# Gate modulation sums tied behind the Strassen sums written ahead of them, and branch B's second factors tied behind attention's output stores

## The chip, the cores and the metric

The kernel runs as one program on one core of one Trainium2 chip. The metric is the device time of one execution in microseconds (us); the median of the runs shown is compared. The engines named below are PE (matrix products), DVE (vector work), ACT (activations, copies), POOL (vector work as well) and SP, which here only issues transfers.

## The reference

One layer of a transformer-like block is computed on 1024 positions of width 1024, all in float32. What matters here, cut down:

```python
c_act = jax.nn.silu(c)
mod = c_act @ ada_w[l] + ada_b[l]
sh1, sc1, g1, sh2, sc2, g2 = jnp.split(mod, 6, axis=-1)
h = rmsnorm(x, ln1_g[l]) * (1.0 + sc1) + sh1
p = h @ w_in[l]
q, k, v, cb, cc, cx, ga, gb = jnp.split(p, split_at, axis=-1)
...
y_a = stick_breaking_attention(q, k, v)
y_b = cb * causal_dwconv(cc * cx, conv_w[l])
merged = (jax.nn.sigmoid(ga) * (y_a @ w_branch_a[l])
          + jax.nn.sigmoid(gb) * (y_b @ w_branch_b[l]))
x = x + g1 * (merged @ w_out[l])
h = rmsnorm(x, ln2_g[l]) * (1.0 + sc2) + sh2
...
x = x + g2 * f
```

The change concerns two things: where in time four of the six vectors of `mod` are summed (they are used only after attention: `g1`, `sh2`, `sc2`, `g2`), and when `y_b` is read back for its product with `w_branch_b`.

## The kernel before, in words

**The gate stage.** Six of the eight parts of `p` (q, cc, cx, cb, gb, ga) are computed here in 24 rounds, called gates here, by one loop (L671 to L745). A gate computes two blocks of 128 output rows by 1024 positions. It uses Strassen's scheme: seven products `p1` to `p7` take the place of eight. Each product is 12 matmuls of 128x512 (L131 to L133: a high part and a low part of each float32 weight), so a gate is 84 matmuls. PE takes them strictly in the order written: p1, p2, p6, p5, p7, p3, p4. The gates run in the order `gates` (L466): section 5 (q) four times; then for each j of 0 to 3 the sections 1, 2 and 0 (cc, cx, cb); then section 4 (gb) four times and section 3 (ga) four times. Counted from 0, gate 13 is section 1 with j=3, and gates 16 and 17 are the first two of section 4.

For each gate SP loads two weight tiles `raw` and `raw2` of 512 KB (L451). POOL makes four combinations of them, `ws` (L136 as a helper, and L682), and ACT and DVE split each factor in two: ACT writes the high part `whi` (L462), DVE the low part `wlo` (L136). The seven products land in PSUM buffers `pj`, of which there are six; DVE adds them up to the four outputs, tiles `c` (L136, the Strassen sums `c11`, `c12`, `c21`, `c22`). A PSUM buffer comes free when its sum has been made. In section 0 the result is multiplied with the convolution's output on POOL and written out by ACT in two parts, `ybt` (L655 to L658).

**The modulation sums.** The generator `mods_later` (L539 to L583) computes the four vectors. Each vector takes eight loads of 512 KB, `ad` (L550), and for each load one DVE instruction that multiplies and sums along the row into a column of `msum` (L565, followed by a short read of the accumulator). The loads are written up to three ahead of the sums, and a quota per gate limits them; their buffers have the tags `tr` and `sq`, two each, shared with `yt`, `ybt` and others of the same gates. After the eight sums of the vector of section 2 (`g1`) and of section 5 (`g2`), DVE adds a bias (`msum += gcol`, L571), and PE spreads the result over the partitions by 16 small matmuls (L578). For the two other vectors DVE writes `mod`. The loop calls `step()` (L660) after each Strassen output: `later()` follows c11, c22, c12 and c21, and in section 1 there is a fifth call at the end of the gate.

The instructions of one engine are issued in an order that a scheduler works out from the written order and its own estimate of when each operand is ready. Before the change a sum may therefore stand on DVE wherever the scheduler believes that its load has landed, also ahead of Strassen sums that were written before it.

**The attention stage.** Per head and block of 128 queries PE computes scores `z` (L846, L847), ACT their sigmoid, DVE a scan `pt` (L856), PE transposes, ACT and DVE split these into `ath` and `atl`, and PE multiplies with v into `o` (L885). ACT writes `o` to an `oy` tile (L889, four buffers), and SP stores it in two transfers to `d_ya` (L893). The factors of each head are loaded by SP in six transfers (L782 to L784: `sqt`, `skh`, `skl`). Between attention's steps PE runs other products as fillers, among them branch B's `y_b @ w_branch_b` (L946 to L948). Its second factors are loaded back in two halves of positions by `load_yb(0)` and `load_yb(1)` (L952 to L959): each makes eight loads of 512 KB `big<-d_yb` on SP. They are written inside `tc.issue_after(lastz[0].ins)`: after the last score matmul written so far.

Of the kernel before, what the change touches and what calls it, by code (L numbers as in the profile page):

```python
# [12 lines left out]
ALU = mybir.AluOpType  # L13
# [9 lines left out]
DH = 64  # L23
# [7 lines left out]
def block_kernel(tc, x, x_t, cols, ada_1, ada_2, ada_row, w_q, w_kv, w_v1, w_cg, w_a, w_b, w_o, w_g, w_u, w_d, out):  # L31
    nc = tc.nc
# [100 lines left out]
            nc.tensor.matmul(ps, wl[:, k, :], fh[:, k, :], start=False, stop=(k == 3))  # L133

    def tt(eng, out, a, b, op):
        eng.tensor_tensor(out=out, in0=a, in1=b, op=op)  # L136


    psA = ExitStack()
# [253 lines left out]
    ml = factors()  # L393
# [40 lines left out]
    for e in range(3):  # L434
        n = d_v[e].shape[0]
# [105 lines left out]
    def mods_later():  # L541

        cab = gp.tile([P, D], F32, name="cabg")
        todo, ahead = [(q, k) for q in range(len(SECS)) for k in range(KT)], ads_

        def load_next():
            if todo and quota[0] > 0:
                quota[0] -= 1
                ad = gp.tile([P, D], F32, tag=("tr", "sq")[len(todo) % 2], bufs=2, name=nm("ad"))
                nc.sync.dma_start(ad, ada_2[todo.pop(0)])  # L550
                ahead.append(ad)

        nc.sync.dma_start(cab, ada_row[0:1, :].broadcast_to([P, D]))
        cs_ = gp.tile([P, D], F32, tag="tr", bufs=2, name=nm("cs"))
        nc.scalar.activation(cs_, cab, AF.Sigmoid)
        for n in range(2):
            tt(nc.vector, cab[:, n * 512:n * 512 + 512], cab[:, n * 512:n * 512 + 512], cs_[:, n * 512:n * 512 + 512], ALU.mult)
        yield
        for q, sec in enumerate(SECS):
            ms = gp.tile([P, 8], F32, tag="msum", bufs=2, name=nm("msum"))  # L560
            for k in range(KT):
                while len(ahead) < 3 and todo and quota[0] > 0:
                    load_next()
                ad = ahead.pop(0)
                nc.vector.tensor_tensor_reduce(out=ad, in0=ad, in1=cab, scale=1.0, scalar=0.0, op0=ALU.mult,  # L565
                                               op1=ALU.add, accum_out=ms[:, k:k + 1])
                yield
            if sec in (3, 4):
                tt(nc.vector, mod[:, sec - 1], ms, acol[:, sec - 1], ALU.add)
                continue  # L570
            e = 0 if sec == 2 else 1  # L571
            tt(nc.vector, ms, ms, gcol[:, e], ALU.add)
            yield
            gb_ = gp.tile([P, D], F32, tag="tr", bufs=2, name=nm("gb"))
            for n in range(2):
                ps = g_ss()
                for i in range(4):
                    nc.tensor.matmul(ps[:, i * P:(i + 1) * P], ms[:, 4 * n + i:4 * n + i + 1].broadcast_to([P, P]), ident,  # L578
                                     start=True, stop=True)
                nc.scalar.activation(gb_[:, n * 512:(n + 1) * 512], ps, AF.Copy)  # L580
            nc.scalar.dma_start(d_g[e], gb_)
            yield
# [77 lines left out]
    def step():  # L660
        if (quota[0] or ads_) and ml_begun:
            ml_begun.append(1)
            next(ml, None)

    uc, ys = {}, {}
    pend, pmm, eq = [], [], end_q()
    with tc.high_priority(), tc.issue_after(last_raw[0].ins):
        nc.sync.dma_start(ft[6].bitcast(F32), d_t[6])
    for g, (sec, j) in enumerate(gates):
        raw, raw2 = raws  # L670
        if g == 7:  # L671
            next(ml)
            ml_begun.append(1)
        p1, p2 = pre[g] if g in pre else (g_prod(g_split(raw[:, :512]), 0), g_prod(g_split(raw[:, 512:]), 1))
        a11, a12, a21, a22 = raw[:, :512], raw[:, 512:], raw2[:, :512], raw2[:, 512:]
        s1, s2_, s3, s4 = (gp2.tile([P, 512], F32, tag=f"ws{q}", bufs=1, name=nm("ws")) for q in range(4))
        with tc.high_priority() if g == 0 else ExitStack():
            tt(nc.gpsimd, s3, a11, a21, ALU.subtract)
            tt(nc.gpsimd, s2_, a22, s3, ALU.subtract)
            w6 = g_split(s2_)  # L680
        tt(nc.gpsimd, s1, a21, a22, ALU.add)
        ws4 = nc.gpsimd.tensor_tensor(out=s4, in0=a12, in1=s2_, op=ALU.subtract)  # L682
        if g + 1 < len(gates):
            raws = two_raw(g + 1)
        c11, c21, c12, c22 = (gp.tile([P, 512], F32, tag=f"c{q}", bufs=2, name=nm("c")) for q in range(4))

        def put(c, m, n):
            if sec == 5:
                pend.append((c, m, n))
            elif sec > 2:  # L690
                nc.scalar.activation(c, c, AF.Sigmoid)
                nc.scalar.dma_start((d_sga, d_sgb)[sec - 3][m, :, n * 512:(n + 1) * 512], c)
            elif sec == 0:
                put_b(c, m, n)
            elif sec == 1:
                ccs[m, n] = c
            elif n == 1 and m >= 4:
                ccs["late"] = c
            else:
                put_u(c, m, n)  # L700
                if n == 0 and m >= 4:
                    put_u(ccs["late"], m, 1)

        quota[0] = (4 if j else 0) if sec == 1 else 3 if sec in (3, 4) and g + 1 < len(gates) else 0
        turn = [0]

        def later():
            if sec == 1 or sec in (3, 4) and turn[0] > 0:
                step()
            turn[0] += 1  # L710
            if len(pmm) > 1 or pmm and not pend:
                sum_q(*pmm.pop(0))
            if pend:
                put_q(*pend.pop(0))
            elif g > 3 and not pmm:
                with tc.issue_after(ws4.ins):
                    next(eq, None)

        nc.scalar.activation(c11, p1, AF.Copy)
        p4 = g_prod(g_split(a22), 3) if g + 1 == len(gates) else None  # L720
        p6 = g_prod(w6, 5)
        tt(nc.vector, c21, p6, c11, ALU.add)
        tt(nc.vector, c11, p2, c11, ALU.add)
        put(c11, j, 0)
        later()
        p5 = g_prod(g_split(s1), 4)
        tt(nc.vector, c12, p5, c21, ALU.add)
        p3 = g_prod(g_split(s4), 2) if g == 0 else None
        p7 = g_prod(g_split(s3), 6)
        tt(nc.vector, c22, p7, c12, ALU.add)  # L730
        put(c22, j + 4, 1)
        later()
        tt(nc.vector, c21, p7, c21, ALU.add)
        p3 = p3 or g_prod(g_split(s4), 2)
        tt(nc.vector, c12, p3, c12, ALU.add)
        put(c12, j, 1)
        later()
        p4 = p4 or g_prod(g_split(a22), 3)
        tt(nc.vector, c21, p4, c21, ALU.add)
        later()  # L740
        put(c21, j + 4, 0)
        if g + 1 == len(gates):
            for _ in eq:
                pass
        if sec == 1:  # L745
            step()
        if g + 1 == len(gates):
            quota[0] = 99
            for _ in ml:
                pass  # L750
# [74 lines left out]
    lastz = [None]  # L825
# [52 lines left out]
    def att_av(h, g):  # L878
        pr, e0 = h // 2, (h % 2) * DH
        vt = vts[h]  # L880
        o = pps.tile([P, 256], F32, tag="o", bufs=1, name=nm("o"))
        for j in range(2 * g + 2):
            c0 = P if j == 2 * g + 1 else 0
            th, tl = ats[h, g, j // 4]
            nc.tensor.matmul(o[:, c0:], vt[:, j, :], th[:, j % 4, c0:], start=(j == 0), stop=False)  # L885
            lastav[0] = nc.tensor.matmul(o[:, c0:], vt[:, j, :], tl[:, j % 4, c0:], start=False, stop=(j == 2 * g + 1))
        yv = bp.tile([P, 256], F32, tag="oy", bufs=4, name=nm("oy"))
        for e in range(2):
            nc.scalar.activation(yv[:, e * P:(e + 1) * P], o[:, e * P:(e + 1) * P], AF.Identity,  # L889
                                 bias=vlast[:, h, 2 * g + e:2 * g + e + 1])  # L890
        hf, c0 = g // 2, (g % 2) * 256
        for e in range(2):
            nc.sync.dma_start(d_ya[hf][pr, e0:e0 + DH, e, c0:c0 + 256], yv[e * DH:(e + 1) * DH])  # L893
        yield None

    NZ, NTR, NPJ, DAV, KQ = 2, 3, 2, 4, 1
# [44 lines left out]
    def mm_ch(ps, w, ah, al, k0=0, k1=KT):  # L941

        for k in range(k0, k1):
# [3 lines left out]
            nc.tensor.matmul(ps, wh, rl_, start=False, stop=False)  # L947
            nc.tensor.matmul(ps, wl, rh_, start=False, stop=(k == KT - 1))  # L948

    yh, yl = [], []  # L950

    def load_yb(n):  # L952
        yh.append(big())
        yl.append(big())
        for k in range(0, KT, 2):
            for e, t in enumerate((yh, yl)):
                with tc.issue_after(lastz[0].ins):
                    nc.sync.dma_start(t[n][:, k:k + 2].bitcast(F32), d_yb[e][n][:, k:k + 2])
                yield  # L959

# [63 lines left out]
    def fill(to):  # L1024
        nonlocal tf
        while tf < to:
            d_ = next(fl, None)
            if d_ is None:
                break
            tf += d_  # L1030
# [630 lines left out]
```

## Time and profile before

| what | value |
|---|---|
| median of 3 runs (lowest to highest) | 1830.23 us (1827.88 to 1831.91) |
| the profiled execution, its own time | 1838.09 us |
| its span in the trace | 1836.3 us |
| mean granted PE clock | 0.994 |
| PE, DVE, ACT, POOL busy, share of the span | 98%, 74%, 43%, 28% |
| SP's transfers (queue q1) | 302.76 MB, 50.7% of 16 DMA engines |
| loads `ad<-ada`, L550 | x32, 512 KB each, 4.6 us to landing (median) |
| loads `raw<-w_cg`, L451 | x40, 512 KB each, 3.8 us to landing (median) |

The profile is of one execution; 1.8 us of its time lie outside the span, and it took 7.9 us more than the median of the runs. Rows of a timeline begin with the start and the duration in us; a bracket at the end names how long the engine had been idle and what released it. In a table of windows each engine has its busy time and, in brackets, the instructions that began in that window; the three last columns are the granted clock of PE, the busy share of the DMA engines and GB/s.

### The profile page before, as it was taken

The page shows a single profiled execution, that of the slowest core. Times are in us where ns is not written, and L with a number is a line of the kernel's source. Part 1 is how long each engine was busy: PE and PEld are TensorE (multiplying, and loading weights), DVE is VectorE, ACT ScalarE, POOL GpSimd, SP SyncE. Part 2 cuts the span into 40 slices and gives each one's busy share as a digit, 9 for nine tenths or more (in the row PEclk, how much of TensorE's full clock was granted, in tenths as well). Part 3 has the DMA queues.
Part 4 walks back from the last instruction along what each step waited for, and adds up shares of the span by engine and source line. Part 5 has one row for each costly group of instructions (what it writes and reads, how often), then busy time and mean ns, then how long its engine had stood idle before and what let it go on. Part 6 is the DMA issues. An engine that isn't in the chain of part 4 may idle for free. (4 is left out here: it accounts for less than half of the span.)

```text
span 1836.3 us, 24702 instructions
## 1 busy us (share of the span) xinstructions
PE 1794.5 (98%) x8781; PEld 1498.3 (82%) x8781; DVE 1352.1 (74%) x1882; ACT 793.9 (43%) x1510; POOL 505.5 (28%) x362
## 2 busy tenths in 40 slices
PE   7999999999989999899999999999999999999999
PEld 4788778878878899788887888877888888878887
DVE  7873877988896448788998655589977788644776
ACT  3452553333334347677776321663444344422321
POOL 0043338533333211342221000105544454200000
PEclk9999999999989999999999999999999999999999
DMA  9687542344484388887775646424534344299876
GB/s 395 196 320 293 184 138 74 119 140 149 129 295 138 118 253 227 255 212 189 176 172 161 231 149 217 134 94 154 204 138 149 129 171 171 104 331 345 283 230 219
DMA packets 164018, 357.48 MB, mean 195 GB/s; under 512 B 15976, under 2 KB 65456, under 8 KB 161720
## 3 DMA queue, kind: packets, MB, share of 16 engines
q1 hardware_dynamic: 133880, 302.76, 50.7%
q10 hardware_dynamic: 29008, 49.48, 7.3%
q0 software_dynamic: 1008, 3.67, 0.5%
q8 instruction: 70, 1.15, 0.3%
q14 instruction: 52, 0.43, 0.1%
HBM read 245.22 MB, written 110.66 MB: 194 GB/s over the span
## 5 line engine op out<-in xcount | busy, mean ns | idle before, releaser
L856 DVE TENSOR_TENSOR_SCAN pt<-pt,mk 128x896 f32<-128x896 f32 (+7 forms) x128 | 189.4, 1480 | 14.5 <-ACT pt L848 14.5
L131 PE MATMUL pj<-big,whi 128*128 128x512 f32 x384 | 150.9, 393 | 2.5 <-DVE c L136 2.5
L133 PE MATMUL pj<-big,wlo 128*128 128x512 f32 x384 | 150.1, 391 | 0.0
L132 PE MATMUL pj<-big,whi 128*128 128x512 f32 x384 | 150.1, 391 | 0.0
L136 DVE TENSOR_TENSOR c<-pj,c 128x512 f32<-128x512 f32 x168 | 111.7, 681 | 43.1 <-PE pj L133 42.8
L136 POOL TENSOR_TENSOR ws<-raw,raw 128x512 f32<-128x512 f32 x44 | 60.8, 1381 | 297.8 <-DMA raw<-w_cg 144.7
L131 PE MATMUL e<-big,whi 128*128 128x512 f32 x352 | 137.5, 391 | 2.0 <-ACT c L1388 1.4
L133 PE MATMUL e<-big,wlo 128*128 128x512 f32 x352 | 137.0, 389 | 0.0
L132 PE MATMUL e<-big,whi 128*128 128x512 f32 x352 | 137.0, 389 | 0.0
L136 DVE TENSOR_TENSOR c<-e,c 128x512 f32<-128x512 f32 x138 | 92.9, 687 | 52.7 <-PE e L133 51.7
L874 DVE TENSOR_TENSOR atl<-tr,ath 128x512 fp32r<-128x512 f32 (+1 forms) x192 | 99.3, 543 | 34.9 <-ACT ath L873 34.6
L1488 PE MATMUL e<-whi,f 128*128 128x512 f32 (+1 forms) x319 | 121.8, 382 | 1.0 <-DMA f<-d_f 1.0
L1489 PE MATMUL e<-wlo,f 128*128 128x512 f32 (+1 forms) x319 | 121.8, 382 | 0.0
L1490 PE MATMUL e<-whi,f 128*128 128x512 f32 (+1 forms) x319 | 121.6, 382 | 0.0
L133 PE MATMUL pj<-ft,wlo 128*128 128x512 f32 x288 | 113.4, 394 | 4.3 <-DVE wlo L136 4.3
L848 ACT ACTIVATE pt<-z,rq 128x512 f32<-128x512 f32 (+1 forms) x192 | 105.0, 584 | 24.6 <-PE z L847 24.4
L131 PE MATMUL pj<-ft,whi 128*128 128x512 f32 x288 | 113.5, 394 | 1.8 <-ACT whi L462 1.6
L132 PE MATMUL pj<-ft,whi 128*128 128x512 f32 x288 | 113.0, 393 | 0.0
L308 PE MATMUL pj<-whi,big 128*128 128x512 f32 x352 | 109.4, 396 | 3.6 <-ACT big L291 3.6
L136 DVE TENSOR_TENSOR wlo<-ws,whi 128x512 fp32r<-128x512 f32 x96 | 84.3, 887 | 31.1 <-ACT whi L462 29.0
L462 ACT ACTIVATE whi<-raw 128x512 fp32r<-128x512 f32 x112 | 69.7, 629 | 86.2 <-PE pj L132 49.1
L132 PE MATMUL e<-rl,whi 128*128 128x512 f32 x264 | 103.3, 391 | 2.2 <-DVE rl L136 2.2
(262 smaller groups left out, 4866.0 us busy)
## 6 DMA issues: line engine op xcount, KB each, us to landing
f<-d_f SPq DMA_DIRECT2D x77, 512.0 KB, 3.6
d_f<-fs SPq DMA_DIRECT2D x70, 512.0 KB, 3.2
raw<-w_cg SPq DMA_DIRECT2D x40, 512.0 KB, 3.8
ad<-ada SPq DMA_DIRECT2D x32, 512.0 KB, 4.6
raw<-w_u SPq DMA_DIRECT2D x26, 512.0 KB, 3.4
raw<-w_g SPq DMA_DIRECT2D x25, 512.0 KB, 3.7
ada<-ada SPq DMA_DIRECT2D x8, 1024.0 KB, 9.6
d_t<-ts SPq DMA_DIRECT2D x16, 512.0 KB, 8.1
```

What stands on the lines that cost most here:

```text
L131: nc.tensor.matmul(ps, wh[:, k, :], fh[:, k, :], start=(k == 0), stop=False)
L132: nc.tensor.matmul(ps, wh[:, k, :], fl[:, k, :], start=False, stop=False)
L133: nc.tensor.matmul(ps, wl[:, k, :], fh[:, k, :], start=False, stop=(k == 3))
L136: eng.tensor_tensor(out=out, in0=a, in1=b, op=op)
L308: nc.tensor.matmul(ps, a, b, start=(k == 0 and q == 0), stop=(k == KT - 1 and q == 2))
L462: nc.scalar.activation(hi, src, AF.Copy)
L848: nc.scalar.activation(pt[:, off + s0:off + s0 + m], z[:, :m], AF.Sigmoid, scale=rq[:, 1, i, h:h + 1])
L856: nc.vector.tensor_tensor_scan(out=pt[:, rev], data0=pt[:, rev], data1=mk[:, rev], initial=1.0, op0=ALU.mult, op1=ALU.max)
L874: nc.vector.tensor_tensor(out=tl[:, :nb, c0:c0 + P], in0=src, in1=th[:, :nb, c0:c0 + P].bitcast(F32), op=ALU.subtract)
L1488: nc.tensor.matmul(o, sh, w[0][:, c], start=(j == 0), stop=False)
L1489: nc.tensor.matmul(o, sh, w[1][:, c], start=False, stop=False)
L1490: nc.tensor.matmul(o, sl, w[0][:, c], start=False, stop=(j == NJ - 1))
```

## The change

First, `step()` runs the next piece of `mods_later` inside `tc.issue_after(at[0].ins)`, where `at[0]` is the Strassen sum written last before the call. Each DVE instruction of that piece now stands behind that sum in DVE's order. The loads are also written at another place: a load is written after the sum that makes room for it, not ahead of the next one. Second, the loads of `load_yb(1)` are tied behind the last store of attention's output that is written (`lastya`, L893), not behind the last score matmul; `load_yb(0)` has no tie any more.

```diff
 def mods_later():
...
+        def fill():
+            while len(ahead) < 3 and todo and quota[0] > 0:
+                load_next()
...
             for k in range(KT):
-                while len(ahead) < 3 and todo and quota[0] > 0:
-                    load_next()
+                if not ahead:
+                    fill()
+                    yield
                 ad = ahead.pop(0)
                 nc.vector.tensor_tensor_reduce(out=ad, in0=ad, in1=cab, scale=1.0, scalar=0.0, op0=ALU.mult,
                                                op1=ALU.add, accum_out=ms[:, k:k + 1])
+                fill()
                 yield
...
 def step():
         if (quota[0] or ads_) and ml_begun:
             ml_begun.append(1)
-            next(ml, None)
+            with tc.issue_after(at[0].ins):
+                next(ml, None)
...
-        tt(nc.vector, c11, p2, c11, ALU.add)
+        at[0] = tt(nc.vector, c11, p2, c11, ALU.add)
...
-        tt(nc.vector, c22, p7, c12, ALU.add)
+        at[0] = tt(nc.vector, c22, p7, c12, ALU.add)
...
-        tt(nc.vector, c12, p3, c12, ALU.add)
+        at[0] = tt(nc.vector, c12, p3, c12, ALU.add)
...
-        tt(nc.vector, c21, p4, c21, ALU.add)
+        at[0] = tt(nc.vector, c21, p4, c21, ALU.add)
...
-            nc.sync.dma_start(d_ya[hf][pr, e0:e0 + DH, e, c0:c0 + 256], yv[e * DH:(e + 1) * DH])
+            lastya[0] = nc.sync.dma_start(d_ya[hf][pr, e0:e0 + DH, e, c0:c0 + 256], yv[e * DH:(e + 1) * DH])
...
 def load_yb(n):
...
-                with tc.issue_after(lastz[0].ins):
+                with tc.issue_after(lastya[0].ins) if n else ExitStack():
                     nc.sync.dma_start(t[n][:, k:k + 2].bitcast(F32), d_yb[e][n][:, k:k + 2])
```

Three places show what this does to the order of the instructions. In the changed kernel L565 is L570, L571 is L577, L578 is L584, and L893, L958 are L900, L966.

The first place is DVE in gate 16, the first gate of section 4. Before, its rows are (`ad` and `msum` are the modulation sums, `c` the Strassen sums, `wlo` the low parts of weights):

```order
L565 ISA ad_4295,msum_3825<-ad_4295,cabg 128x1024
L565 ISA msum_3825 128x1
L136 TENSOR_TENSOR ybt_4177<-c_4067,ybt_4177 128x512
L136 TENSOR_TENSOR wlo_4323<-raw_4064,whi_4322 128x512
L565 ISA ad_4453,msum_3825<-ad_4453,cabg 128x1024
L565 ISA msum_3825 128x1
L565 ISA ad_4479,msum_4501<-ad_4479,cabg 128x1024
L565 ISA msum_4501 128x1
L136 TENSOR_TENSOR c_4234<-pj_4238,c_4233 128x512
L136 TENSOR_TENSOR wlo_4361<-raw_4229,whi_4360 128x512
L565 ISA ad_4293,msum_3825<-ad_4293,cabg 128x1024
L565 ISA msum_3825 128x1
```

After it, the same stretch of the same gate reads (numbers of buffers differ by one):

```order
L136 TENSOR_TENSOR wlo_4322<-raw_4063,whi_4321 128x512
L136 TENSOR_TENSOR ybt_4127<-c_4068,ybt_4127 128x512
L136 TENSOR_TENSOR c_4233<-pj_4237,c_4232 128x512
L136 TENSOR_TENSOR wlo_4360<-raw_4228,whi_4359 128x512
L136 TENSOR_TENSOR c_4232<-pj_4203,c_4232 128x512
L136 TENSOR_TENSOR c_4234<-pj_4258,c_4233 128x512
L136 TENSOR_TENSOR ybt_4152<-c_4067,ybt_4152 128x512
L136 TENSOR_TENSOR wlo_4383<-ws_4377,whi_4382 128x512
L136 TENSOR_TENSOR wlo_4433<-ws_4378,whi_4432 128x512
L136 TENSOR_TENSOR c_4235<-pj_4276,c_4234 128x512
L570 ISA ad_3830,msum_3825<-ad_3830,cabg 128x1024
L570 ISA msum_3825 128x1
```

Four sums that stood around gate 16's first Strassen sum have gone from there; the first sum of this gate now stands behind its fourth Strassen sum. Of the 24 sums of the last three vectors 20 stood close together in gates 16 to 18; they are now spread over the gates up to the last, three to a gate.

The second place is the bias of the first vector (`msum_2779`) in gate 13. Before, DVE made it in gate 10, behind the vector's last sum (`ad_3276`):

```order
L136 TENSOR_TENSOR c_3252<-pj_3223,c_3252 128x512
L136 TENSOR_TENSOR c_3254<-pj_3283,c_3253 128x512
L565 ISA ad_3276,msum_2779<-ad_3276,cabg 128x1024
L565 ISA msum_2779 128x1
L136 TENSOR_TENSOR msum_2779<-msum_2779,cst 128x8
```

After the change the bias stands on DVE in gate 13, behind that gate's c11 (`c_3735`) and all that stands ahead of it:

```order
L136 TENSOR_TENSOR ybt_3679<-c_3569,ybt_3679 128x512
L136 TENSOR_TENSOR wlo_3855<-raw_3731,whi_3854 128x512
L136 TENSOR_TENSOR c_3736<-pj_3740,c_3735 128x512
L136 TENSOR_TENSOR wlo_3930<-ws_3888,whi_3929 128x512
L136 TENSOR_TENSOR c_3735<-pj_3706,c_3735 128x512
L136 TENSOR_TENSOR msum_2779<-msum_2779,cst 128x8
```

The matmuls that spread this vector stand on PE in gate 13 in both kernels; before they stood between the last matmul of p7 and the first of p3, and now, as PE's rows of the changed kernel show, behind the fifth matmul of p3 (`pj_3811`):

```order
L133 MATMUL pj_3778<-ft_1519,wlo_3775 128x512
L131 MATMUL pj_3811<-big_148,whi_3807 128x512
L132 MATMUL pj_3811<-big_217,whi_3807 128x512
L133 MATMUL pj_3811<-big_148,wlo_3808 128x512
L131 MATMUL pj_3811<-big_148,whi_3807 128x512
L132 MATMUL pj_3811<-big_217,whi_3807 128x512
L584 MATMUL tr_3793<-dm,msum_2779 128x128 x4
L584 MATMUL tr_3799<-dm,msum_2779 128x128 x4
L133 MATMUL pj_3811<-big_148,wlo_3808 128x512
```

The bias moved three gates later on DVE, while its reader on PE moved by five matmuls. The bias of the vector of section 5 moved in the same way into the last gate, where its reader is.

The third place is SP in the attention stage, at the loads of branch B's second half (`big_6764`, `big_6765`). Before:

```order
L958 DMA big_6764<-d_yb_71 128x1024
L985 DMA d_v_2_69<-vs_1220_6328 128x2x128
L958 DMA big_6765<-d_yb_73 128x1024
L958 DMA big_6764<-d_yb_71 128x1024
L958 DMA big_6765<-d_yb_73 128x1024
L893 DMA d_ya_74<-oy_6718 64x256 x2
L958 DMA big_6764<-d_yb_71 128x1024
L958 DMA big_6765<-d_yb_73 128x1024
L958 DMA big_6764<-d_yb_71 128x1024
L958 DMA big_6765<-d_yb_73 128x1024
L451 DMA raw_8146<-w_b 128x1024
L893 DMA d_ya_75<-oy_6803 64x256 x2
```

After:

```order
L900 DMA d_ya_74<-oy_6718 64x256 x2
L966 DMA big_6764<-d_yb_71 128x1024
L451 DMA raw_8146<-w_b 128x1024
L900 DMA d_ya_75<-oy_6803 64x256 x2
L789 DMA sqt_6858<-d_q_63 64x1024
L790 DMA skh_6859<-d_k_65 64x8x128
L791 DMA skl_6860<-d_k_66 64x8x128
L789 DMA sqt_6858<-d_q_64 64x1024
L790 DMA skh_6859<-d_k_65 64x8x128
L791 DMA skl_6860<-d_k_66 64x8x128
L900 DMA d_ya_74<-oy_6853 64x256 x2
L966 DMA big_6765<-d_yb_73 128x1024
```

One of the eight loads stays in its place; the other seven come behind the six loads of the next head, three of them at once, two more each behind a later store, and the last two together behind the loads of one head more. The eight loads of the first half, `load_yb(0)`, keep their places in the order.

More of the change, by code (lines that the diff above doesn't have):

```diff
@@ L135, in tt @@
     def tt(eng, out, a, b, op):
-        eng.tensor_tensor(out=out, in0=a, in1=b, op=op)
+        return eng.tensor_tensor(out=out, in0=a, in1=b, op=op)
     psA = ExitStack()
@@ L662, in step @@
             ml_begun.append(1)
-            next(ml, None)
-    uc, ys = {}, {}
+            with tc.issue_after(at[0].ins):
+                next(ml, None)
+    uc, ys, at = {}, {}, [None]
     pend, pmm, eq = [], [], end_q()
@@ L948, in mm_ch @@
             nc.tensor.matmul(ps, wl, rh_, start=False, stop=(k == KT - 1))
+    lastya = [None]
     yh, yl = [], []
```

## The prediction

> **What bounds the kernel now.** I read the page first, then the windows of the two stages that the change touches, then the timelines of the engines inside the odd windows.
>
> ```profile
> PE 1794.5 (98%) x8781; PEld 1498.3 (82%) x8781; DVE 1352.1 (74%) x1882; ACT 793.9 (43%) x1510; POOL 505.5 (28%) x362
> 480.00:500.00 20.00, 20.00 (x90) 16.54 (x89) 18.85 (x23) 6.24 (x11) 8.97 (x6) 1.00 0.46 143
> 500.00:520.00 20.00, 14.74 (x55) 11.38 (x54) 16.52 (x27) 5.33 (x9) 7.70 (x4) 0.87 0.93 329
> 520.00:540.00 20.00, 20.00 (x80) 16.28 (x79) 20.00 (x32) 6.55 (x12) 7.98 (x4) 0.88 0.85 291
> 740.00:760.00 20.00, 19.48 (x126) 16.91 (x126) 18.56 (x22) 13.91 (x35) 10.40 (x6) 1.00 0.79 224
> 760.00:780.00 20.00, 15.67 (x84) 13.12 (x83) 11.00 (x17) 9.53 (x24) 1.28 (x1) 0.85 1.02 300
> ```
>
> PE is busy 98% of the span, so time can only be won where it stands still or runs at a lower clock. In the gate stage a full window holds 90 matmuls, 20.00 / 90 = 0.222 us each. The windows from 500 and from 520 hold 55 and 80: 35 + 10 = 45 matmuls too few, or 10.0 us. In attention the window from 760 lacks 20.00 - 15.67 = 4.3 us of PE and runs at 0.85, another 0.15 x 20 = 3.0 us: 7.3 us. These two places are what the change can win. Everything else that it does must be free or costs.
>
> **The gate stage's two stalls.** The timelines of PE, DVE, POOL and SP in the windows from 500 on say where the 10.0 us come from:
>
> ```profile
> 507.86 0.80 PE L131 MATMUL pj<-big,whi 128*128 128x512 f32 x1 [2.04 <-DVE c L136]
> 518.83 0.79 PE L133 MATMUL pj<-ft,wlo 128*128 128x512 f32 x1 [3.22 <-DVE wlo L136]
> 505.97 1.23 DVE L565 CUSTOM_DVE_ANT_0 ad<-ad,cabg 128x1024 f32<-128x1024 f32 x1 [2.49 <-DMA ad<-ada]
> 507.12 0.69 DVE L136 TENSOR_TENSOR c<-pj,c 128x512 f32<-128x512 f32 x1
> 508.71 1.98 POOL L136 TENSOR_TENSOR ws<-raw,raw 128x512 f32<-128x512 f32 x1 [11.44 <-DMA raw<-w_cg]
> 497.30 3.61 SPq L550 DMA_DIRECT2D ad<-ada  x3
> 501.28 0.33 SPq L451 DMA_DIRECT2D raw<-w_cg  x1
> 524.54 0.54 PE L131 MATMUL pj<-ft,whi 128*128 128x512 f32 x1
> L565 DVE CUSTOM_DVE_ANT_0 ad<-ad,cabg x32: 1205/1217/2345, 330.9 to 550.8; 128x1024 f32<-128x1024 f32 x32
> ```
>
> At 507.86 PE had been idle for 2.04 us, released by a Strassen sum that DVE made at 507.12; DVE had stood 2.49 us before a modulation sum whose load had not landed, with the Strassen sum behind it. At 518.83 PE had been idle for 3.22 us: the second weight tile was issued at 501.28, behind three `ad` loads, and POOL began its combinations at 508.71 after 11.44 us of waiting. After each stall PE goes on at half its clock for a while: the matmul at 524.54 is the first of the second stall that is shorter than 0.63 us. So 5.3 us are idle time, and 10.0 - 5.3 = 4.7 us the slower clock.
>
> After the change no `ad` sum stands ahead of gate 16's first Strassen sum, and the second weight tile of gate 17 is issued ahead of all four `ad` loads of that stretch. I take both stalls as gone: -10.0 us, with 0 as the other bound. What is late next is DVE itself: a gate of section 4 then has three sums of 1.217 us in each 84 x 0.222 = 18.7 us. In the window from 480 DVE is busy 18.85 of 20 us, but with section 0's work in it, which these gates no longer have; the cover is thin and is a rival below.
>
> **Two small waits earlier.**
>
> ```profile
> 387.59 0.50 PE L131 MATMUL pj<-big,whi 128*128 128x512 f32 x1 [0.46 <-DVE c L136]
> 395.32 0.50 PE L133 MATMUL pj<-ft,wlo 128*128 128x512 f32 x1 [1.13 <-DVE wlo L136]
> ```
>
> They are of the same kind, 1.6 us together. Whatever of them goes is swallowed by the next term, whose end is set by DVE and a store, not by when PE gets there. I count 0, bounds -1.6 and 0.
>
> **The new wait: the bias in gate 13.** This is the cost that I expect. The first vector's bias was made on DVE here, long before use, and its 16 spreading matmuls ran without waiting:
>
> ```profile
> 391.63 1.14 DVE L136 TENSOR_TENSOR msum<-msum,cst 128x8 f32<-128x8 f32 x1
> 441.29 1.95 PE L578 MATMUL tr<-dm,msum 128*128 128x128 f32 x16
> ```
>
> Now the bias stands behind c11 of gate 13. At that point DVE runs late in the trace of before:
>
> ```profile
> 441.86 0.63 ACT L655 ACTIVATE ybt<-c 128x512 fp32r<-128x512 f32 x1 [3.37 <-DMA d_yb<-ybt]
> 442.52 1.31 DVE L136 TENSOR_TENSOR ybt<-c,ybt 128x512 fp32r<-128x512 f32 x1 [1.73 <-ACT ybt L655]
> 443.75 1.21 DVE L565 CUSTOM_DVE_ANT_0 ad<-ad,cabg 128x1024 f32<-128x1024 f32 x1
> 444.24 0.63 ACT L462 ACTIVATE whi<-raw 128x512 fp32r<-128x512 f32 x1 [1.26 <-DVE ybt L136]
> 446.65 0.69 DVE L136 TENSOR_TENSOR c<-pj,c 128x512 f32<-128x512 f32 x1
> 447.26 0.68 DVE L136 TENSOR_TENSOR wlo<-ws,whi 128x512 fp32r<-128x512 f32 x1
> 447.86 1.28 DVE L136 TENSOR_TENSOR c<-pj,c 128x512 f32<-128x512 f32 x2
> ```
>
> ACT waited 3.37 us for a store of an earlier `ybt` tile; that held DVE's `ybt`, which ended at 442.52 + 1.31 = 443.83, and ACT's `whi`, which ended at 444.24 + 0.63 = 444.87. The change takes away the two `ad` sums that followed, and leaves four instructions ahead of the bias: `wlo` from 444.9 (it needs that `whi`), a Strassen sum, a `wlo` and c11. By their starts in these rows (446.65, 447.26, 447.86) each takes 0.6 us, so c11 ends at 444.9 + 4 x 0.6 = 447.3, and the bias at about 447.6. PE wants the result five matmuls of p3 after p7, whose end is 441.29: 441.29 + 5 x 0.227 = 442.4. PE takes its work in order, so p3, p4 and the next gate are queued behind the spreading matmuls: 447.6 - 442.4 = 5.2 us idle. For the slower clock afterwards the nearest row is the 3.22 us stall: half its clock until 524.54, which is 5.7 us at half speed, so 2.9 us. Sum +8.1 us, bounds 0 (DVE not late) and 10 (1.14 us for the bias as at 391.63, PE earlier by the small waits).
>
> The trace shows that 2.04 us of idle are already enough to halve the clock: the matmul at 507.86 took 0.80 us. The Trainium skill ("TensorE: Matmul & The Clock Gate", Part 1: The HAM clock gate) says that the clock falls after an idle window of about 3.4 us and comes back after about 3.4 us of work. Its first figure disagrees with the row at 507.86, where 2.04 us were enough; by its second figure the new wait would cost 5.2 + 1.7 = 6.9 us instead of 8.1, and the sum below would be 1.2 us lower.
>
> **The bias in the last gate.**
>
> ```profile
> 646.65 2.01 DVE L136 TENSOR_TENSOR c<-pj,c 128x512 f32<-128x512 f32 x3 [1.43 <-PE pj L133]
> 649.17 1.95 PE L578 MATMUL tr<-dm,msum 128*128 128x128 f32 x16
> ```
>
> The last sum (1.217 us) and the bias fall between these Strassen sums: 646.65 + 0.6 + 1.2 + 0.6 + 0.2 = 649.25 against 649.17. I take +0.3 us, bounds 0 and 1.2.
>
> **Attention's stall.** The timelines of SP, ACT and PE:
>
> ```profile
> 754.70 3.73 SPq L958 DMA_DIRECT2D big<-d_yb  x4
> 761.11 1.09 SPq L893 DMA_DIRECT2D d_ya<-oy  x2
> 766.38 0.57 SPq L783 DMA_DIRECT2D skh<-d_k  x1
> 769.17 0.63 ACT L889 ACTIVATE oy<-o,vlast 128x128 f32<-128x128 f32 x2 [4.08 <-DMA d_ya<-oy]
> 774.84 0.80 PE L846 MATMUL z<-skh,sqt 128*128 128x512 f32 x1 [3.23 <-DMA d_ya<-oy]
> ```
>
> Eight loads of 512 KB go out ahead of the stores and of the next head's factors. ACT waits 4.08 us for an `oy` buffer, and PE 3.23 us for the scores; `skh`, issued at 766.38, is among the loads that the scores need. After the change only one of the eight stands ahead of the six factor loads. I take the 7.3 us of the window as gone; bounds 0 and -8. The cover for the seven loads that move back is the time until branch B's second half reads them, the first one here:
>
> ```profile
> 782.69 0.39 PE L946 MATMUL pj<-big,whi 128*128 128x512 f32 x1
> ```
>
> The factor loads would go out some 3 us earlier, the next loads of `d_yb` at about 767, and 7.4 us (from 501.28 to 508.71, the slowest 512 KB load above) puts them at 775. The last two go behind another head's loads; their readers come last in the same product.
>
> **Sum.** -10.0 + 0 + 8.1 + 0.3 - 7.3 = -8.9 us. The profiled execution took 1838.09 us and would take 1829.2; it lies 7.9 us above the median of the runs, 1830.23, which would become 1821.3. What a measurement can tell from no change is about 0.2%, 3.7 us.
>
> **Rivals.**
>
> *The new wait does not open.* DVE's lag in gate 13 hangs on one store of 3.37 us; if this lands in time, or if the DVE is ahead by the two sums and more, the 8.1 us fall away: -17.0, 1813.2. For: no PE wait stands near 441 in before. Against: the `ybt` chain ahead of it is not edited. Chance 0.22.
>
> *The burst in attention moves and does not shrink.* In the window from 760 the DMA engines were busy throughout (1.02) and in the one before at 0.79. The seven loads carry the same bytes and may now hold back the stores behind which they stand. If the 7.3 us come back there, -1.6 is left: 1828.6. The Trainium skill ("DMA: Bandwidth & Descriptors", Issuing engines are not separate DMA queues) says that transfers of all issuers share the same 16 engines and interleave, so a new order alone gives no more room; no run shows yet whether the room around is enough. Chance 0.15.
>
> *The sums hold the weight tiles (slower).* On SP the second weight tile of each later gate now stands behind `ad` loads, and these wait for buffers that a sum frees, which in turn waits for a Strassen sum. The load that came late in before was issued at 501.28 and used from 508.71, and PE then waited 3.22 us; so from about 508.71 - 3.22 = 505.5 on, each microsecond is PE's. If a sum keeps SP back by that much in two of the seven later gates, it costs 2 x (3.2 + 2.9) = 12.2 us: +3.3, 1833.5; more gates cost 6.1 each. Against: the loads come one after another and DVE has spare time in these gates. Chance 0.13.
>
> The order of the instructions shows the edit in effect, so that it does nothing is no rival. The forecast keeps 0.50.
>
> **Range and chances.** The first rival's 1813 with 2 us of its own is the lower end, 1811; the upper end takes the second rival and the attention term at its bound 0 with a new wait of 10: 1830.23 - 10.0 + 10 + 1.2 = 1831.4, so 1832. Faster by over 0.2% are the forecast, the first rival and a little over half of the second: 0.80, less 0.02 for the forecast's own unlucky ends: 0.78. Within 0.2%: the rest of the second and half of the third, 0.13. Slower: 0.09.
>
> **What would show it.** Right: windows of 20 us between 480 and 640 with 90 matmuls and clock 1.00; a PE wait of about 5 us at L584 near 442, released by DVE `msum`; no wait at L846 near 767 and a window there above 19 us. Wrong: L584 without a wait (the first rival), `oy` still waiting 4 us for `d_ya` (the second), or PE waits for `wlo` between 520 and 640 with POOL waiting for `raw` (the third).

## The result and the profile after

The change took 1826.69 us (median of 20 runs, 1822.26 to 1832.85) against 1830.02 us of the kernel before (20 runs, 1827.88 to 1835.29). The ratio is 0.9976, with a 95% interval of 0.9966 to 0.9985: 4.4 us faster, between 2.7 and 6.2; the two medians themselves lie 3.3 us apart. The forecast was 1821.3, or 8.9 us faster. The two profiled executions lie 9.6 us apart, 1838.09 and 1828.48 us. So there are two things to explain: where the 9.6 us of the profiles came from, and why the medians show half of it or less.

Two windows of the profile before that matter here, and then six of the profile after, with the columns as before:

```profile
380.00:400.00 20.00, 18.27 (x78) 14.16 (x77) 16.06 (x25) 5.10 (x9) 6.62 (x4) 1.00 0.49 174
780.00:800.00 20.00, 19.58 (x127) 17.37 (x127) 16.86 (x19) 13.63 (x33) 7.44 (x5) 0.98 0.80 214
```

```profile
380.00:400.00 20.00, 20.00 (x90) 16.40 (x89) 14.08 (x21) 4.58 (x8) 6.78 (x5) 1.00 0.44 162
440.00:460.00 20.00, 14.78 (x63) 12.79 (x64) 12.38 (x20) 6.52 (x12) 3.86 (x3) 0.83 0.44 157
500.00:520.00 20.00, 20.00 (x90) 16.55 (x89) 15.44 (x25) 8.93 (x15) 5.56 (x4) 1.00 0.83 258
520.00:540.00 20.00, 20.00 (x90) 16.56 (x89) 12.91 (x21) 7.28 (x12) 5.42 (x4) 1.00 0.72 241
760.00:780.00 20.00, 20.00 (x135) 18.09 (x134) 17.74 (x23) 14.22 (x36) 8.24 (x5) 1.00 0.86 296
780.00:800.00 20.00, 17.98 (x108) 15.38 (x107) 15.95 (x19) 11.25 (x28) 2.13 (x3) 0.91 1.06 255
```

The windows from 500 and 520 are full, and so are the one from 380 and the one from 760. In their place stand two new holes, from 440 and from 780. The first is the bias; ACT, DVE and PE there:

```profile
439.53 0.63 ACT L661 ACTIVATE ybt<-c 128x512 fp32r<-128x512 f32 x1 [1.95 <-DMA d_yb<-ybt]
442.12 0.69 DVE L136 TENSOR_TENSOR wlo<-raw,whi 128x512 fp32r<-128x512 f32 x1 [1.07 <-ACT whi L462]
444.41 0.68 DVE L136 TENSOR_TENSOR c<-pj,c 128x512 f32<-128x512 f32 x1
445.01 0.15 DVE L136 TENSOR_TENSOR msum<-msum,cst 128x8 f32<-128x8 f32 x1
445.22 3.78 PE L584 MATMUL tr<-dm,msum 128*128 128x128 f32 x16 [5.65 <-DVE msum L136]
449.22 0.63 PE L131 MATMUL pj<-big,whi 128*128 128x512 f32 x1
450.41 0.39 PE L131 MATMUL pj<-big,whi 128*128 128x512 f32 x1
```

As in the profile before, ACT has waited for a store of an earlier `ybt` tile, and DVE runs late behind it. PE stands still for 5.65 us until DVE has made the bias at 445.16, and the 16 spreading matmuls then take 3.78 us instead of 1.95; at 450.41 the clock is whole again. The second hole, PE, ACT and SP in attention:

```profile
785.99 0.47 PE L853 MATMUL z<-skh,sqt 128*128 128x512 f32 x1 [1.15 <-issue]
787.05 0.50 PE L854 MATMUL z<-skl,sqt 128*128 128x512 f32 x1 [0.59 <-DMA skl<-d_k]
789.49 0.80 PE L954 MATMUL pj<-big,whi 128*128 128x512 f32 x1 [0.29 <-DMA big<-d_yb]
787.46 0.63 ACT L896 ACTIVATE oy<-o,vlast 128x128 f32<-128x128 f32 x2 [2.89 <-DMA d_ya<-oy]
781.50 1.73 SPq L966 DMA_DIRECT2D big<-d_yb  x2
```

The last two loads of `d_yb` are issued at 781.50, behind the factors of the head after next. PE waits 1.15 us before a score matmul, where the profile shows no releaser, then 0.59 us for those factors and 0.29 us for such a load. ACT waits 2.89 us for a store of `oy`. Where attention lost 7.3 us in the window from 760, the window from 780 now loses 20.00 - 17.98 = 2.0 us of PE and 0.09 x 20 = 1.8 us by the clock.

The ends of the stages add up to the difference of the profiles:

```profile
644.36 2.02 PE L584 MATMUL tr<-dm,msum 128*128 128x128 f32 x16
```

Before, the same matmuls began at 649.17: the gate stage is 4.8 us shorter. The spans differ by 1836.3 - 1826.6 = 9.7 us, so attention and all behind it gave the other 4.9.

### The profile page after: what moved, and what is told of

It is laid out like the page before. It is cut to its first block, busy times and chain, and to the rows that moved or that the text cites. A ratio compares the mean times of both kernels' runs of the same rounds, so it can differ in the third digit from the quotient of the medians.

```text
span 1826.6 us, 24690 instructions
## 1 busy us (share of the span) xinstructions
PE 1789.8 (98%) x8781; PEld 1495.8 (82%) x8781; DVE 1343.7 (74%) x1882; ACT 794.5 (43%) x1510; POOL 499.1 (27%) x362
## 3 DMA queue, kind: packets, MB, share of 16 engines
q8 instruction: 70, 1.15, 0.3%
## 5 line engine op out<-in xcount | busy, mean ns | idle before, releaser
L462 ACT ACTIVATE whi<-ws 128x512 fp32r<-128x512 f32 x96 | 57.9, 626 | 110.1 <-POOL ws L136 78.2
```

The source lines that it names most:

```text
L462: nc.scalar.activation(hi, src, AF.Copy)
```

## The experiments

The theory to be tested: both stalls were removed as the order says, the bias gives a new wait that costs about 8 us in every execution, and the profiled execution of before was one with longer stalls than most. The rivals: the gain is given back somewhere else in every execution (A below), or one of the two stalls is usually shorter (B and C).

**The kernel before again, and the two halves by themselves.** The first of these runs is the kernel before without an edit. The second is the change with the loads as they were:

```diff
-                with tc.issue_after(lastya[0].ins) if n else ExitStack():
+                with tc.issue_after(lastz[0].ins):
```

The third is the kernel before with the loads of the change (and `lastya` set at the store, as there):

```diff
-                with tc.issue_after(lastz[0].ins):
+                with tc.issue_after(lastya[0].ins) if n else ExitStack():
```

> The kernel before, profiled once more. The change measured about 4 us by the medians, while the two profiled executions lie 9.6 us apart (1838.09 and 1828.48), and the execution on which the prediction's sum was made lay 7.9 us above the median of its kernel. Theory A, the terms of the sum hold in every execution and something else gives the time back: this profile shows the same places again, 135 matmuls in the two windows from 500 to 540 and about 7 us lost in the window from 760. Theory B, the profiled execution had longer gate stalls than others: more than 150 matmuls in the windows from 500 to 540, attention's loss still about 7 us. Theory C, it had a longer stall in attention than others: 135 matmuls again, and less than 4 us lost in the windows from 760 to 800.

> The modulation sums tied as in the change, branch B's loads as before. Theory A (terms as predicted): -10.0 + 8.1 + 0.3, so 1.6 us faster than before. Theory B (the gate stalls are usually shorter): about 3 us slower, because the new wait for the bias costs more than the stalls did. Theory C: 1.6 us faster, as A. In each of them the wait at the spreading matmuls in gate 13 is there, 5 to 6 us.

> Branch B's loads tied as in the change, the modulation sums as before. Theory A and theory B: about 7 us faster than before. Theory C (attention's stall is usually shorter): 2 to 3 us faster.

The kernel before took 1836.87 us in its second profile, where 23 runs on the same chip have a median of 1833.50. Its windows show both places again, which are the signs of theory A and not those of B and C. But this execution was once more slower than most (19 of the 23 were quicker), so it does not show what a quick one looks like:

```profile
500.00:520.00 20.00, 12.76 (x53) 9.70 (x52) 15.58 (x24) 4.73 (x8) 7.81 (x4) 0.94 0.91 307
520.00:540.00 20.00, 20.00 (x80) 16.27 (x80) 20.00 (x32) 7.15 (x12) 7.78 (x4) 0.88 0.89 307
760.00:780.00 20.00, 16.58 (x87) 13.81 (x87) 11.80 (x18) 10.27 (x26) 1.32 (x2) 0.84 1.03 297
```

The gate half alone measured 0.9980 (0.9967 to 0.9993), 3.7 us faster (1.3 to 6.1), where A and C said 1.6 and B said 3 slower. The load half alone measured 0.9978 (0.9965 to 0.9991), 4.0 us faster (1.7 to 6.4), where A and B said 7 and C 2 to 3. So the intervals leave out B's numbers and A's 7, and hold C's; but no profile showed C's sign. Taken singly the halves give 7.7 us, together 4.4; by the times alone, with intervals this wide, that does not show an overlap. The gate half's own profile shows one:

```profile
440.00:460.00 20.00, 14.49 (x60) 12.47 (x60) 12.46 (x20) 6.80 (x12) 4.23 (x3) 0.83 0.45 163
760.00:780.00 20.00, 18.92 (x123) 16.50 (x122) 16.07 (x20) 12.39 (x33) 8.43 (x4) 1.00 0.88 220
765.98 0.50 PE L853 MATMUL z<-skh,sqt 128*128 128x512 f32 x1 [0.44 <-DMA skh<-d_k]
767.06 0.50 PE L854 MATMUL z<-skl,sqt 128*128 128x512 f32 x1 [0.58 <-DMA skl<-d_k]
```

With the eight loads of `d_yb` where they had always been, attention loses 1.1 us of PE and no clock. The wait for the bias is there in full. The load half's own profile, in turn, has the gate stage's two stalls (54 and 82 matmuls in the windows from 500) and a full window from 760.

**The biases early.** This is the whole change with each bias made on DVE right behind the last sum of its vector. On PE the spreading matmuls of gate 13 go back to where they stood before the change; no other instruction of PE, DVE, POOL or SP changes its place.

```diff
                 fill()
+                if k == KT - 1 and sec in (2, 5):
+                    tt(nc.vector, ms, ms, gcol[:, 0 if sec == 2 else 1], ALU.add)
                 yield
...
-            tt(nc.vector, ms, ms, gcol[:, e], ALU.add)
```

> The whole change, but each of the two biases is added on DVE right behind the last sum of its vector, three gates earlier for the first; nothing else moves on DVE, and the spreading matmuls go back to the end of p7. If the new wait costs what the prediction put on it, this is about 8 us faster than the change: 12 us faster than before, if the change is 4 us faster. The rival, that PE's wait hides a lateness of DVE or of the weights which then shows in the next gate: less than 3 us faster than the change, with waits of PE for wlo or c between 440 and 480.

> The change as it is, once more, on the chip of the next two. About 4 us faster than before, with the wait of 6 us for the bias.

> The change with early biases, on the same chip as the change. The wait for the bias with its slower clock was priced at 8.1 us: 8 us faster than the change. It measured 12.8 us below before on one chip, the change 4.4 on another.

The first of these measured 0.9930 (0.9913 to 0.9947). For a comparison on one chip the change and this kernel were run there together: the change 1826.86 us, 0.9971 (0.9960 to 0.9982); early biases 1817.84 us, 0.9921 (0.9905 to 0.9937); the kernel before 1831.37. So the early bias is worth 9.0 us where 8.1 were expected. Rows of this kernel's profile on that chip, and then of the change's: the window from 440, the spreading matmuls of the last gate, and the window in attention that lost most:

```profile
440.00:460.00 20.00, 20.00 (x91) 16.60 (x91) 16.84 (x25) 7.70 (x14) 7.03 (x5) 1.00 0.52 176
636.27 2.02 PE L585 MATMUL tr<-dm,msum 128*128 128x128 f32 x16
760.00:780.00 20.00, 18.88 (x125) 16.66 (x124) 17.48 (x21) 13.77 (x34) 9.33 (x5) 1.00 0.87 260
```

```profile
440.00:460.00 20.00, 14.71 (x65) 12.79 (x66) 12.20 (x20) 6.77 (x12) 3.94 (x3) 0.83 0.50 180
643.80 2.02 PE L584 MATMUL tr<-dm,msum 128*128 128x128 f32 x16
780.00:800.00 20.00, 18.30 (x109) 15.90 (x108) 15.25 (x19) 11.79 (x29) 2.61 (x3) 0.91 1.05 268
```

The hole is gone, and in the gates behind it no wait of PE came in its place: DVE's lateness in gate 13 had cost nothing as long as nothing on PE needed it. The 9.0 us are not the wait alone, though. The two profiles lie 1827.38 - 1816.84 = 10.5 us apart, and only 643.80 - 636.27 = 7.5 us of that at the end of the gate stage. Most of the rest is attention's second hole, 1.7 us of PE and 1.8 us by the clock with the change, 1.1 us and no clock with early biases. SP issues the same transfers in the same order in both, so the place of the last two loads does not make that hole by itself; why it shrinks was not tested.

**Early biases without the load half.** The same kernel, with the loads of `d_yb` as in the kernel before:

```diff
-                with tc.issue_after(lastya[0].ins) if n else ExitStack():
+                with tc.issue_after(lastz[0].ins):
```

> The modulation sums tied, the biases early, and branch B's loads as before: the kernel with early biases without the load half. That kernel was 12.8 us faster than before. Theory P, the load half keeps its own worth (4 us, as measured alone on the kernel before): this one is about 8.5 us faster than before, and its profile shows 3 us and more lost between 740 and 790. Theory Q, the load half removes a stall that the gate half already shrinks, since attention then reaches the loads in another phase: 11 to 13 us faster than before.

> Early biases without the load half, on the same chip as the kernel with it. If the load half adds nothing on top of the gate half (theory Q), within 1.5 us of the kernel before this one. If it keeps a worth of its own (theory P, 12.8 against 10.2 on two chips), 2.5 us and more slower.

It measured 0.9944 (0.9932 to 0.9956) on the one chip, 10.2 us faster than before. On the other, beside the kernel with the load half, it took 1819.02 us against 1817.84, 0.9934 (0.9915 to 0.9953). The first of these lies between the two forecasts (8.5 for P, 11 to 13 for Q), with an interval from 8.1 to 12.4 us that reaches both; the second, on one chip with its rival, is what Q said: on top of the gate half the load half is worth 1.2 us there, and the two intervals overlap. So Q fits better, and a small worth of the load half is not ruled out. Its window in attention, in the second of the two profiles:

```profile
740.00:760.00 20.00, 18.97 (x123) 16.74 (x122) 16.97 (x22) 12.26 (x32) 1.28 (x1) 1.00 1.06 325
760.00:780.00 20.00, 19.88 (x133) 17.75 (x132) 17.07 (x21) 14.73 (x37) 9.29 (x5) 1.00 0.82 221
```

One microsecond is lost where the kernel before lost seven, with the same order of attention's loads.

**Branch B's loads in pairs.** Early biases, and all eight loads written so that none stands behind the factors of the head after next:

```diff
                     nc.sync.dma_start(t[n][:, k:k + 2].bitcast(F32), d_yb[e][n][:, k:k + 2])
-                yield
+                if not n or e:
+                    yield
```

> The whole change with early biases, and branch B's second factors written in pairs, so that all eight loads stand on SP ahead of the second next head's factors and not the last two behind them. The profile of the kernel with early biases shows PE waiting for skl (1.31 between starts) and for a load of d_yb (1.17) near 780. If these come from the last two loads, 2 us faster than with early biases, so about 14.5 us faster than before; if the loads are simply moved into the path of the stores again, as before the change, PE waits of 3 us and a lower clock come back near 765 and it is 3 to 5 us slower than with early biases.

It measured 0.9947 (0.9932 to 0.9963), 9.7 us faster than before: no better than the kernel without the load half on the same chip (10.2), and 3 us short of what early biases alone had measured on another (12.8), as its second forecast said. The wait for `skl` and `d_yb` near 780 went, and another came, on ACT and PE:

```profile
781.33 0.63 ACT L897 ACTIVATE oy<-o,vlast 128x128 f32<-128x128 f32 x2 [7.16 <-DMA d_ya<-oy]
782.76 0.58 PE L893 MATMUL o<-ath,vt 128*128 128x256 f32 x1 [4.90 <-ACT ath L881]
```

With six loads at once the stores of `oy` are late again, as they were before the change, one head further on.

**Is attention's stall fixed to the program?** The kernel before and the gate half, each profiled once more, and the kernel before with one load of v's weights later on SP:

```diff
-                with tc.issue_after(lastld[0].ins) if e else ExitStack():
+                with tc.issue_after((vst if j else lastld)[0].ins) if e else ExitStack():
                     raw = g_raw(w_v1[e, j])
...
-                nc.sync.dma_start(d_v[1 + e][:, 1:, i].rearrange("r p d -> p r d"), vs.rearrange("p (r d) -> p r d", d=P))
+                vst[0 if (e, i) == (0, 4) else 1] = nc.sync.dma_start(d_v[1 + e][:, 1:, i].rearrange("r p d -> p r d"), vs.rearrange("p (r d) -> p r d", d=P))
```

> The kernel before, profiled a third time. Two profiles of it had 135 and 133 matmuls in the windows from 500 to 540 (180 without a stall) and 84 and 87 in the window from 760. If the stalls are fixed to the program, the numbers are within 3 of these. If they come and go with the execution, at least one of the two places shows half the loss or less.

> The gate half alone, profiled a second time. Its first profile lost only 1.1 us in the window from 760, with branch B's loads as before, at a clock of 1.00. If attention's stall comes and goes with the execution, this profile may show 3 us and more lost there and a clock below 0.95; if the gate half removes it, the window has again over 18.5 us of PE.

> The kernel before, with one load of v's weights (512 KB, about 100 us ahead of attention's stall) four rows later on SP; PE's order is unchanged. The gate half moves the same load by one row, and its two profiles lost 1.1 and 1.3 us in the window from 760 instead of 7. If this place on SP decides attention's stall, it shrinks here too: over 18 us of PE in the window from 760, clock above 0.95, and 3 to 5 us faster than before. If the phase in which attention begins decides it, which the gate stage's stalls set, the window stays at about 16 us of PE and a clock of 0.85, and the time is within 1.5 us of before.

The kernel before took 1836.85 us in its third profile, and both stalls are there a third time; the second profile of the gate half (1827.73 us) again has almost none in attention. In this order, the window from 760:

```profile
760.00:780.00 20.00, 15.82 (x85) 12.99 (x83) 10.94 (x17) 10.23 (x26) 1.28 (x1) 0.83 1.05 303
```

```profile
760.00:780.00 20.00, 18.71 (x123) 16.38 (x122) 16.80 (x21) 12.21 (x31) 7.43 (x4) 1.00 0.82 207
```

With the one load moved, the window has 17.50 us of PE at a clock of 0.91, a little over half the loss, but the time did not follow: 1.0008 (0.9993 to 1.0023). This run is inconclusive: neither the place of that load nor the phase alone explains what the gate half does to attention's stall.

**Profile against median.** The three profiled executions of the kernel before took 1838.09, 1836.87 and 1836.85 us, on chips where its medians were 1830.02, 1833.50 and 1829.83. The 21 runs beside the last four kernels go from 1828.56 us, at a mean granted clock of 0.998, to 1838.88 us at 0.994. The difference in clock alone, 0.004 x 1834 = 7.3 us, is most of these 10.3 us; over all 21 the two go together less closely, and one run at 0.998 took 1833.27 us. The change, beside them, stayed between 1825.13 and 1828.04 in 10 runs (in its first 20 it had ranged from 1822.26 to 1832.85), and early biases between 1816.84 and 1819.54 in 6. Thus the kernel before scatters by 10 us, and all three of its profiles caught an execution in the upper part: two were slower than all 20 and all 11 runs beside them. That is not so for every kernel: with the load moved, early biases and the halves, the profiled executions lie between 2.8 us below and 3.1 us above their medians. Why it is so for the kernel before stays open.

The clock does show that a quick execution of the kernel before had less of these stalls. In the first profile the windows from 500, 520, 760 and 780 lost (0.13 + 0.12 + 0.15 + 0.02) x 20 = 8.4 us by the clock; in the second the three windows shown lost (0.06 + 0.12 + 0.16) x 20 = 6.8 us. A run whose mean clock is 0.998, rounded, lost at most 0.0025 x 1827 = 4.6 us by it from beginning to end. In which of the two stalls the half speed was shorter, and whether PE also stood still for less time, was not seen, since none of the quick executions left a trace.

## Why the prediction was right in its direction and too large

**The gate stage's two stalls: right in the profile.** Both windows hold 90 matmuls. The kernel with early biases and the old loads puts a lower price on them against the runs of the kernel before: 10.2 and 12.1 us for these stalls, the small waits and the part of attention's stall that went with them.

**The two small waits: too low.** They are gone as well: 78 matmuls became 90 in the window from 380. That is 12 x 0.222 = 2.7 us, where the prediction put 0 and at most 1.6. PE therefore wanted the bias not at 442.4 but at 445.22 - 5.65 = 439.6. The prediction let the wait that follows swallow what was won here, because its end was taken as set by DVE and a store; but that end came 2.4 us earlier too, so most of the 2.7 us stayed won.

**The new wait: right, and the best part of the working.** Its mechanism and its place were forecast from rows of a trace that shows no such wait, and its price nearly: 8.1 us forecast, 7.5 us in the pair of profiles, and 9.0 us between the medians with part of attention's second hole in it. That the idle time fits so well, 5.2 us forecast and 5.65 found, is partly luck. ACT had its buffer at 439.53 and not at 441.86, DVE was ready at 445.16 and not at 447.6, and PE came 2.8 us earlier: two shifts that the prediction did not have and that nearly cancel.

**The bias in the last gate: nothing.** The matmuls there did not wait (2.02 us in the row at 644.36); 0.3 us had been allowed.

**Attention's stall: right in the profile, wrong as a gain of its own.** The 7.3 us of the window from 760 went, 3.8 came back in the window from 780, where 0.8 had been lost before (19.58 us of PE at 0.98). That is close to the second rival, at part of its price: a store of `oy` is waited for again, 2.89 us where it was 4.08, and the last two loads stand behind another head's factors. But early biases, with the same order on SP, lost 1.1 us and no clock there, so the order alone is not the cause. The prediction had waved these two loads through with "their readers come last in the same product". And the term was not free to be added: the gate half alone takes 6 of the 7.3 us, by a cause that stays open.

**The third rival** did not come: no PE wait for `wlo` stands between 520 and 640.

**The sum by stages.** The sum was -8.9 us against -9.6 in the profiles, but that is luck in part. Its terms for the gate stage give -10.0 + 0 + 8.1 + 0.3 = -1.6 us, and 4.8 were won there, the difference mostly from the small waits; its term for attention gives 7.3, and 4.9 were won there and behind it. The two misses nearly cancel.

**The step that failed** is the last line of the sum: "it lies 7.9 us above the median of the runs, 1830.23, which would become 1821.3". It carries the whole sum over to the median, as if the 7.9 us had nothing to do with what the change removes. The runs speak against that: the profiled executions of the kernel before lie 3.4 to 8.1 us above their medians, those of the change 1.8 and 0.5 us; and by their clocks the quick executions of the kernel before had less of the stalls. The cost that the change adds, the wait for the bias, was there in all four profiles that could have it (5.4 to 6.2 us). So the gains had to be cut on the way to the median, and the cost not. By how much is an estimate made afterwards: with up to 7.9 us off the 17.3 us of stalls, the sum for the median lies between -8.9 and -1.0, which holds the 4.4. That this is the whole of the difference is argued and not shown, since no quick execution of the kernel before was traced. The range, down to the other cases, held the time.

## What to carry to other kernels

When the profiled execution lies well above the median, look at what the change removes: if it is stalls, the execution may be slow because of them, and only a part of each may be there in the median run, while here a new wait that hangs on the program's order was there in every profile. Compare the stage sums with the stages and not only the total: here two misses made a good total. When instructions are tied behind others to keep them out of the way, follow the last one of the chain to its reader on the bottleneck engine; here one add of 0.15 us, three gates later than before, took back two thirds of the gain (9.0 of 13.5 us by the medians on one chip), and the cure was to leave that one where it was. Two edits that remove stalls on the same transfer queue should be measured singly and together before both are kept.

## What the runs showed of the hardware

The same wait at the same place lowers the clock in one execution and not in another. In the first profile of the kernel before, the row at 507.86 shows 2.04 us of idle and the matmul behind it at 0.80 us. In its second and third profiles PE waited longer at that place, and the matmul behind took 0.50 us, at full clock:

```profile
508.51 0.50 PE L131 MATMUL pj<-big,whi 128*128 128x512 f32 x1 [2.72 <-DVE c L136]
```

```profile
508.72 0.50 PE L131 MATMUL pj<-big,whi 128*128 128x512 f32 x1 [3.37 <-DVE c L136]
```

So the prediction's "2.04 us of idle are already enough" is true of its trace, but 2.04 us is no threshold. The wait of 1.13 us at 395.32 and the gate half's two waits of 0.44 and 0.58 us left the clock at 1.00 too. A stall cut from 3.2 us to 1.0 saved twice here: the idle time, and the 3.0 us that the slower clock cost in the window from 760.

How long the half speed lasts behind a wait varies as well, in the same program at the same place: until 450.41 in the profile of the change, 5.2 us after the wait's end, and in its second profile until the row at 449.14 below, 3.8 us. The loss by the clock in the window from 440 is nevertheless the same in both, (1 - 0.83) x 20 = 3.4 us, that is 6.8 us at half speed; the rest of it, about 1.6 and 3.0 us, lay inside the wait, where it costs nothing. The Trainium skill ("TensorE: Matmul & The Clock Gate", Part 1: The HAM clock gate) says that the window which decides this runs freely and does not start with the work; these profiles agree with that.

```profile
445.30 3.78 PE L584 MATMUL tr<-dm,msum 128*128 128x128 f32 x16 [5.44 <-DVE msum L136]
448.73 0.58 PE L133 MATMUL pj<-big,wlo 128*128 128x512 f32 x1
449.14 0.40 PE L131 MATMUL pj<-big,whi 128*128 128x512 f32 x1
```
